# A planned order with corrected durations, two more weight slots, and one unit for the exponentials of an SSD group

## The chip, the cores and the metric

The kernel runs on one core of a Trainium2 chip. The metric is the device time of one execution in microseconds (us); the median of three runs of the kernel before is 1147.33 us (1146.54 to 1148.89). The engines are named as the profile names them: PE (TensorE, matmuls), DVE (VectorE), ACT (ScalarE), POOL (GpSimd), and SP, whose queue issues every DMA of this kernel.

## The reference, cut to what matters

One sequence of 256 tokens with 1024 features passes through two layers in fp32. A layer is a SwiGLU feed-forward block, a mixer, and a second feed-forward block, each followed by a layer norm. The mixer of the first layer ("hyb") joins a gated delta rule with an mLSTM; that of the second ("ssd") is a chunked state-space scan.

```python
for l in range(DEPTH):
    x = _layer_norm(DN_ALPHA * x + 0.5 * _swiglu(x, ffn_pre_w_gate[l], ...))
    mix = _hybrid_mixer(x, ...) if l % 2 == 0 else _ssd_mixer(x, ...)
    x = _layer_norm(DN_ALPHA * x + mix, ...)
    x = _layer_norm(DN_ALPHA * x + 0.5 * _swiglu(x, ffn_post_w_gate[l], ...))
```

Three pieces of the mixers matter below. The delta rule solves with a unit lower triangular matrix per head and chunk, `triangular_solve(lower + eye, rhs)`. The mLSTM gates its output, `o_b = sigmoid(mo) * h`. The scan needs for each head the decay between all pairs of positions of a chunk, `seg = exp(where(causal, a_cum[i] - a_cum[j], -inf))`, the decay to the chunk's end `d_end`, and `e_cum = exp(a_cum)`.

## The kernel before, in words

**Numbers.** All weights are fp32 in memory. A block of weights arrives as a tile `raw` (128 rows of 1024 or 1040 columns, about half a megabyte); ACT rounds it into `hi` and DVE forms the rest `lo`; each product is then three matmuls (hi with hi, lo with hi, hi with lo) of 128x256 to 128x512 columns. So every block costs one cast on ACT and one subtraction on DVE beside its matmuls on PE.

**Who sets the order.** The class `Plan` records every operation of the program and, in `order()` (L354), plays a list scheduler over them with durations of its own (`_cost`, L269), due times (`rank`, L321) and a model of the DMA queue. What it finds becomes the instruction order of each engine, and also gives each tile its slot: tiles of the kind `m4`, which hold `raw`, `hi`, `lo`, and most wide intermediates, share `NSLOT` slots (L33). `emit` (L476) then issues all of them from one line, so in the profile every instruction stands at L488 and is told from others by its tiles. Engines run their queues strictly in that order; a table of numbers in the scheduler therefore changes the program without a change in the mathematics.

**The hyb mixer around the triangular solve.** `k_dot` gives the products of keys; DVE multiplies them into `Ls` (two halves, 16 instructions). SP writes `Ls` to scratch memory (`scrdl`) and reads it back as `ab`, the 16x16 diagonal blocks, 64 rows each (L1084 to L1085). `block_inverse` (L1283) inverts them on DVE, and begins with a product of `ab` with a constant mask and a difference from the identity, both columns of the constant array `cst`. Beside it runs the mLSTM: its weights `mE` are multiplied on PE with `mv`, DVE divides by the denominator `md` and gates with `sg` into `my`, and PE transposes `my` for the output projection (written `tr<-ident,my`). In the recorded order DVE does the block inverse ahead of `md` and `my`.

**The ssd mixer.** There are four groups of eight heads. `decays(gi)` (L1417) loads, for a group, two tiles `abc` (a half of the sequence each, broadcast over the partitions from scratch), and ACT turns them into decays: eight `Relu` instructions with a per-head bias per tile (so that what would be above the diagonal is cut off), then `Exp`. Two small exponentials belong to it: `sea` (once) and `sde` (per group). ACT holds one table of functions at a time: `Exp` needs another than `silu`, and the instruction ACT_TABLE_LOAD stands wherever the order changes from one to the other. `chunk(gi)` (L1469) multiplies `abc` with `cb` (from the feature-major `bf` and `cf`, which come out of a convolution `cv` and a silu), transposes `xf`, forms `xd`, `xe` and `y` on DVE, multiplies `xe` into a state, which ACT copies to `hst`, and adds the product of `hst` with `cf`.

Of the kernel before, what the change touches and what calls it, by code (L numbers as in the profile page):

```python
# [19 lines left out]
P = 128  # L20
D = 1024
S = 256
# [10 lines left out]
NSLOT = 40  # L33
# [7 lines left out]
C_EYE16 = 896  # L41
C_LOW16 = 1152
C_N = 1408


def _const_array():
# [9 lines left out]
    c[:, C_LOW16:C_LOW16 + 256] = np.tril(np.ones((16, 16), np.float32), -1).reshape(1, 256)  # L56
    c[:, C_EYE16:C_EYE16 + 256] = np.eye(16, dtype=np.float32).reshape(1, 256)
# [3 lines left out]
SB_SLOTS = {"m4": (NSLOT, WMAX), "m2": (6, 512), "m1": (6, 256), "tiny": (12, 16), "tiny96": (12, 96)}  # L61
# [12 lines left out]
class Buf:  # L74


    def __init__(self, n, tag, shape, dtype, name):
# [6 lines left out]
        self.ops = []  # L84
        self.place = None
# [99 lines left out]
class Plan:  # L185
# [83 lines left out]
    def _cost(self, op, method, a, k):  # L269
# [12 lines left out]
        elif q == "SP":  # L282
# [5 lines left out]
            op.rate = 410 if isinstance(src, bass.AP) and not src.tensor.name.startswith("scr") else 300  # L288
        else:
# [20 lines left out]
            elif q == "ACT":  # L310
                op.busy += 180 + .85 * n + 60 * scal - LAG["ACT"] + (186 if "accum_out" in k else 0)
# [38 lines left out]
    MARGIN, LEAD = 1000, 0  # L350
# [3 lines left out]
    def order(self):  # L354
# [18 lines left out]
        dma = 0.0  # L373
# [12 lines left out]

        def start(o, q):
            t = max(ready[o, q], clock[q])
            if o.news:
# [23 lines left out]
        while len(out) < len(ops):  # L413
            best = None
            for q in QUEUES:
# [4 lines left out]
                now = [(o.prio + 2 * switch(o, q), o.n, t, o) for t, o in can if t <= t0]  # L420
                mine = min(now)
                for p, n, t, o in sorted((o.prio + 2 * switch(o, q), o.n, t, o) for t, o in can if t > t0):
# [24 lines left out]
            if q == "SP":  # L447
                first = max(dma, t + busy)
                dma = first + max(350, o.bytes / o.rate)
                end = dma + 2000 + self.MARGIN * o.raw  # L450
# [6 lines left out]
            o.done, o.begun, o.on = end, t, q  # L457
            out.append(o)
# [32 lines left out]
class Net:  # L491
# [92 lines left out]
    def consts(self):  # L584
# [7 lines left out]
        self.ones = self.one([32, S], F32, name="ones")  # L592
        nc.gpsimd.memset(self.ones, 1.0)
# [277 lines left out]
    def hyb(self, g, b, last=False):  # L871
# [24 lines left out]
        ones = self.ones[0:8]  # L896

# [38 lines left out]
        with hp():  # L936
            sin = t96(12, "sin")
            V.tensor_copy(sin[:, :, 0:8], gt[:, :, 8:16])
            V.tensor_scalar_mul(sin[:, :, 8:12], gt[:, :, 20:24], -1.0)
# [15 lines left out]
            rw = self.m4([8, 4, S], nm="hrows")  # L955
            for half in range(2):
# [130 lines left out]
        mq = self.m4([P, 2, S], nm="mq")  # L1087
# [3 lines left out]
        mk = self.m4([P, 2, S], nm="mk")  # L1091
# [3 lines left out]
        for pr in range(2):  # L1095
            for q in range(2):
# [5 lines left out]
                qk = V.tensor_mul(e, e, ps[:, 0:3 * P])  # L1102
        with hp():
# [533 lines left out]
```

## Time and profile before

| | |
|---|---|
| median of 3 runs | 1147.33 us |
| profiled execution, device time | 1146.67 us |
| its span in the profile | 1144.9 us |
| PE busy | 1112.7 us (97%) |
| DVE busy | 758.5 us (66%) |
| ACT busy | 587.9 us (51%) |
| mean granted clock of PE | 0.995 |

The profiled execution lies 0.66 us below the median, and 1.8 us of its device time lie outside its span. Busy time is time in which an engine had an instruction under way; since matmuls overlap in the pipeline, a busy PE need not be at its best rate. The granted clock is 1.00 at 2.4 GHz and 0.50 at 1.2 GHz. Times in rows count from the start of the span.

### The profile page before, as it was taken

How to read it: one execution, taken by the hardware profiler on the slowest of the kernel's cores; microseconds unless marked ns; L12 is line 12 of the kernel's file. 1: busy time of each engine (PE TensorE's matmuls, PEld its weight loads, DVE VectorE, ACT ScalarE, POOL GpSimd, SP SyncE). 2: the span in 40 equal slices, each digit the busy share in tenths (PEclk: the TensorE clock that was granted, in tenths of full speed). 3: DMA queues.
4: the chain of work that ended last, by engine and by line, in shares of the span. 5: the costliest groups of instructions: out<-in, count | busy, mean ns of one | idle time of the engine just before them, and what ended most of it. 6: DMA issues, size and time to landing. Idle time of an engine off the chain costs nothing.

```text
span 1144.9 us, 19783 instructions
## 1 busy us (share of the span) xinstructions
PE 1112.7 (97%) x8118; PEld 1041.5 (91%) x8118; DVE 758.5 (66%) x1242; ACT 587.9 (51%) x890; POOL 26.2 (2%) x53
## 2 busy tenths in 40 slices
PE   7999999998999999999999999999999999999996
PEld 7999998998998999999899999899998779999995
DVE  6945456787969955455865545696788889655425
ACT  6755443593423544344354444379889636444410
POOL 0000000000000000000000000000011220000000
PEclk9999999998999999999999999999999999999999
DMA  9766554648424555565465555465545446655601
GB/s 358 288 212 205 196 183 133 191 171 214 186 102 159 197 190 192 191 206 174 148 223 200 188 197 187 134 217 187 185 146 178 149 163 243 218 172 187 212 19 37
DMA packets 75955, 210.02 MB, mean 183 GB/s; under 512 B 13580, under 2 KB 26328, under 8 KB 75864
## 3 DMA queue, kind: packets, MB, share of 16 engines
q1 hardware_dynamic: 75864, 208.76, 54.3%
q8 instruction: 63, 1.03, 0.4%
q14 instruction: 28, 0.23, 0.1%
HBM read 204.23 MB, written 4.50 MB: 182 GB/s over the span
## 4 chain that ended last, share of the span: by engine, by line
PE 81%; DVE 8%; ACT 6%; DMA 3%; issue 1%; SPq 0%; DVEq 0%; ACTq 0%
PE gu L488 46%; PE acc L488 32%; PE tr L488 3%; DVE cv L488 2%; DMA raw<-in_wgu 2%; DVE lo L488 2%; ACT L488 2%; ACT abc L488 1%; DVE x L488 1%; ACT cv L488 1%; DMA ab<-scrdl 1%; ACT Ls L488 1%; ACT hi L488 0%; DVE ry L488 0%; DMA x<-in_x 0%
## 5 line engine op out<-in xcount | busy, mean ns | idle before, releaser
L488 DVE TENSOR_TENSOR lo<-raw,hi 128x1024 fp32r<-128x1024 f32 (+2 forms) x358 | 428.8, 1216 | 145.0 <-ACT hi L488 141.4
L488 ACT CAST hi<-raw 128x1024 fp32r<-128x1024 f32 (+2 forms) x358 | 370.1, 1045 | 203.0 <-DMA raw<-in_wgu 125.1
L488 PE MATMUL gu<-xl,hi 128*128 128x256 f32 x1216 | 341.9, 281 | 0.0
L488 PE MATMUL gu<-xh,hi 128*128 128x256 f32 x1216 | 341.2, 281 | 0.0
L488 PE MATMUL gu<-xh,lo 128*128 128x256 f32 x1216 | 341.1, 281 | 0.0
L488 PEld LDWEIGHTS gu<-xh,hi 128*128 128x128 f32 x1216 | 229.0, 188 | 1.0
L488 PEld LDWEIGHTS gu<-xl,hi 128*128 128x128 f32 x1216 | 228.9, 188 | 1.1
L488 PEld LDWEIGHTS gu<-xh,lo 128*128 128x128 f32 x1216 | 229.1, 188 | 0.0
L488 PE MATMUL acc<-hi,h 128*128 128x512 f32 (+1 forms) x748 | 228.7, 381 | 0.0
L488 PEld LDWEIGHTS acc<-hi,h 128*128 128x128 f32 x748 | 138.1, 188 | 27.5
L488 PE MATMUL acc<-lo,h 128*128 128x512 f32 (+1 forms) x374 | 142.1, 380 | 0.0
L488 ACT ACTIVATE sg<-gu 128x256 f32<-128x256 f32 (+1 forms) x100 | 35.9, 359 | 183.3 <-PE gu L488 183.1
L488 DVE TENSOR_TENSOR hf<-sg,gu 128x256 f32<-128x256 f32 (+1 forms) x100 | 38.7, 388 | 108.2 <-ACT sg L488 108.0
L488 PE MATMUL acc<-xh,hi 128*128 128x256 f32 x320 | 92.7, 290 | 0.0
L488 PE MATMUL acc<-xl,hi 128*128 128x256 f32 x320 | 90.5, 283 | 0.0
L488 PE MATMUL acc<-xh,lo 128*128 128x256 f32 x320 | 90.2, 282 | 0.0
L488 PEld LDWEIGHTS acc<-lo,h 128*128 128x128 f32 x374 | 70.3, 188 | 13.1
L488 PE MATMUL acc<-hi,xh 128*128 128x260 f32 x224 | 64.0, 286 | 0.0
L488 PE MATMUL acc<-hi,xl 128*128 128x260 f32 x224 | 63.4, 283 | 0.4 <-DVE xl L488 0.4
L488 PE MATMUL acc<-lo,xh 128*128 128x260 f32 x224 | 63.3, 283 | 0.0
L488 PEld LDWEIGHTS acc<-xh,hi 128*128 128x128 f32 x320 | 61.0, 190 | 0.6 <-issue 0.2
L488 DVE TENSOR_TENSOR h<-hf,h 128x256 fp32r<-128x256 f32 x76 | 32.3, 425 | 44.0 <-ACT h L488 44.0
(272 smaller groups left out, 1445.5 us busy)
## 6 DMA issues: line engine op xcount, KB each, us to landing
raw<-in_wgu SPq DMA_DIRECT2D x176, 512.0 KB, 5.0
raw<-in_wd SPq DMA_DIRECT2D x88, 512.0 KB, 5.8
raw<-in_ssd_fm SPq DMA_DIRECT2D x24, 512.0 KB, 5.7
raw<-in_ssd_tm SPq DMA_DIRECT2D x16, 520.0 KB, 4.5
raw<-in_hyb_fm SPq DMA_DIRECT2D x16, 512.0 KB, 5.2
raw<-in_ssd_out SPq DMA_DIRECT2D x16, 512.0 KB, 5.7
raw<-in_hyb_tm SPq DMA_DIRECT2D x12, 520.0 KB, 4.4
raw<-in_hyb_out SPq DMA_DIRECT2D x8, 512.0 KB, 6.8
```

Of the source, the lines that this page charges most:

```text
L488: getattr(engines[o.on], method)(*map(real, a), **{x: real(v) for x, v in k.items()})
```

## The change

The planner gets other numbers: how long scratch transfers take by the size of their pieces, a model in which SP's transfers land one behind the other, a charge for ACT's scalar operands, a larger margin for weights, and a wait for a PSUM bank that another engine still uses. `NSLOT` goes from 40 to 42. Room for that comes from the constants: the 16x16 identity and mask leave `cst` and become an input of their own, `cst16`, loaded on SP into a tile `c16` shortly before the block inverse; the constant tile of ones becomes two small ones that POOL fills where they are used; `mq` and `mk` share a tile. And in `decays`, the exponentials of a group (both halves, `sde`, and `sea` in the first group) are one unit that ACT runs without anything between, with the product `de * dt` behind it. No matmul is added or removed.

```diff
-NSLOT = 40
+NSLOT = 42
...
-C_EYE16 = 896
-C_LOW16 = 1152
-C_N = 1408
+C_N = 896
...
+def _const16():
+
+    c = np.stack([np.eye(16, dtype=np.float32), np.tril(np.ones((16, 16), np.float32), -1)])
+    return np.broadcast_to(c.reshape(1, 512), (P, 512)).copy()
...
-SB_SLOTS = {"m4": (NSLOT, WMAX), "m2": (6, 512), "m1": (6, 256), "tiny": (12, 16), "tiny96": (12, 96)}
+SB_SLOTS = {"m4": (NSLOT, WMAX), "m2": (6, 512), "m1": (6, 256), "tiny": (12, 16), "tiny96": (11, 64)}
...
-            op.rate = 410 if isinstance(src, bass.AP) and not src.tensor.name.startswith("scr") else 300
+            far = [v for v in (out, src) if isinstance(v, bass.AP)][0]
+            if far.tensor.name.startswith("scr"):
+                piece = 4 * far.ap[-1][1]
+                op.rate = 82 if piece <= 64 else 228 if isinstance(src, View) else 291
...
+            for b in o.banks:
+
+                for e, end in b.seen.items():
+                    if e != q:
+                        t = max(t, end + HAND[e][q])
...
-        ones = self.ones[0:8]
-
...
-            V.tensor_scalar_mul(sin[:, :, 8:12], gt[:, :, 20:24], -1.0)
+            neg = V.tensor_scalar_mul(sin[:, :, 8:12], gt[:, :, 20:24], -1.0)
...
+            ones = self.m1([8, S], nm="ones")
+            with self.plan.behind(neg):
+                G.memset(ones, 1.0)
...
-        mq = self.m4([P, 2, S], nm="mq")
+        mqk = self.m4([P, 4, S], nm="mqk")
+        mq = mqk[:, 0:2]
...
-        mk = self.m4([P, 2, S], nm="mk")
+        mk = mqk[:, 2:4]
...
+        c16 = self.m2([P, 512], nm="c16")
+        with self.plan.behind(qk):
+            DQ(c16, self.ap["cst16"])
         with hp():
-            self.block_inverse(ab, c, dd)
+            self.block_inverse(ab, c16, dd)
...
-        ea = t32(1, "sea")
-        A.activation(ea[:, 0, :], nam[:, 1, :], AF.Exp, scale=-1.0)
-        ea = ea[:, 0, :]
+        ea = t32(1, "sea")[:, 0, :]
         de = t32(1, "sde")[:, 0, :]
         M = {}
 
         def decays(gi):
+            sl = slice(gi * 8, gi * 8 + 8)
             for half in range(2):
                 bc = self.m4([P, 8, P], nm="abc")
                 DQ(bc, ds_[half][gi * 8:gi * 8 + 8, :].partition_broadcast(P))
                 if half == 0:
-                    sl = slice(gi * 8, gi * 8 + 8)
                     V.tensor_add(de[:, sl], bc[:, :, P - 1], nam[:, 0, sl])
-                    A.activation(de[:, sl], de[:, sl], AF.Exp)
-                    V.tensor_mul(de[:, sl], de[:, sl], dt[:, 0, sl])
                 for r in range(8):
                     h = gi * 8 + r
                     A.activation(bc[:, r, :], bc[:, r, :], AF.Relu, scale=-1.0, bias=pam[:, half, h:h + 1])
-                A.activation(bc, bc, AF.Exp, scale=-1.0)
                 M[gi, half] = bc
+            with self.plan.group():
+                if gi == 0:
+                    A.activation(ea, nam[:, 1, :], AF.Exp, scale=-1.0)
+                A.activation(de[:, sl], de[:, sl], AF.Exp)
+                for half in range(2):
+                    A.activation(M[gi, half], M[gi, half], AF.Exp, scale=-1.0)
+            V.tensor_mul(de[:, sl], de[:, sl], dt[:, 0, sl])
```

The program after has 22 ACT_TABLE_LOAD instructions, where before it had 38; 24 of those before and 10 of those after stand in the ssd mixer. SP has one DMA more, POOL one memset more.

**First place: SP behind the products `Ls` in hyb.** Before, SP's queue reads (`scrdl` is `Ls` on its way out, `ab` the diagonal blocks on their way in, one for each half, `raw` a block of weights):

```order
111 L488 DMA scrdl_65<-Ls_2580 128x8x128
112 L488 DMA scrdl_66<-Ls_2684 128x8x128
113 L488 DMA raw_2904<-in_hyb_fm 128x1024
114 L488 DMA raw_2922<-in_hyb_fm 128x1024
115 L488 DMA ab_2924<-scrdl_65 64x16x16
116 L488 DMA raw_2983<-in_hyb_fm 128x1024
117 L488 DMA ab_2924<-scrdl_66 64x16x16
118 L488 DMA raw_3009<-in_hyb_fm 128x1024
119 L488 DMA raw_3051<-in_hyb_fm 128x1024
```

After, where `c_441` is the new tile `c16`:

```order
113 L507 DMA scrdl_65<-Ls_2633 128x8x128
114 L507 DMA scrdl_66<-Ls_2696 128x8x128
115 L507 DMA raw_2918<-in_hyb_fm 128x1024
116 L507 DMA ab_2927<-scrdl_65 64x16x16
117 L507 DMA c_441_2938<-in_cst 128x512
118 L507 DMA raw_2982<-in_hyb_fm 128x1024
119 L507 DMA ab_2927<-scrdl_66 64x16x16
120 L507 DMA raw_3018<-in_hyb_fm 128x1024
121 L507 DMA raw_3074<-in_hyb_out 128x1024
```

Behind the two `scrdl` one block of weights stands ahead of the first `ab` and not two; between the two `ab` stand the new constant and one block. On DVE three `gbc` and three `mE` multiplications that stood ahead of `Ls` now stand behind it, and the block inverse still stands ahead of `my`.

**Second place: PE at the transposes of `my` in hyb.** Before:

```order
1854 L488 MATMUL tr_3118<-mv_339_1966,mE_2662 128x129 x2
1855 L488 MATMUL tr_3123<-mv_339_1966,mE_2740 128x129 x2
1856 L488 MATMUL tr_3133<-mv_339_1966,mE_2662 128x129 x4
1857 L488 MATMUL tr_3145<-ident,my_3141 128x128
1858 L488 MATMUL tr_3148<-mv_339_1966,mE_2740 128x129
1859 L488 MATMUL tr_3145<-ident,my_3141 128x128
1860 L488 MATMUL tr_3148<-mv_339_1966,mE_2740 128x129 x2
1861 L488 MATMUL tr_3145<-ident,my_3141 128x128 x2
1862 L488 MATMUL tr_3148<-mv_339_1966,mE_2740 128x129
1863 L488 MATMUL acc_3168<-xh,hi_2877 128x256
1864 L488 MATMUL acc_3168<-xl,hi_2877 128x256
```

After (the left-out rows repeat the three products once more):

```order
1858 L507 MATMUL tr_3120<-mv_339_1952,mE_2669 128x129 x2
1859 L507 MATMUL tr_3124<-mv_339_1952,mE_2734 128x129 x2
1860 L507 MATMUL tr_3132<-mv_339_1952,mE_2669 128x129 x4
1861 L507 MATMUL tr_3146<-mv_339_1952,mE_2734 128x129 x4
1862 L507 MATMUL acc_3163<-xh,hi_2843 128x256
1863 L507 MATMUL acc_3163<-xl,hi_2843 128x256
1864 L507 MATMUL acc_3163<-xh,lo_2916 128x256
...
1868 L507 MATMUL tr_3173<-ident,my_3157 128x128 x4
```

All twelve products with `mE` and six matmuls of the next weights now stand ahead of the first transpose of `my`; before, four of these products stood among and behind the transposes, and the weights came last.

**Third place: ACT in the ssd mixer, from the decays of the second group to the copy `hst` of the first.** Before:

```order
601 L488 ACT_TABLE_LOAD
602 L488 ACTIVATE sde<-sde 128x8
603 L488 ACT_TABLE_LOAD
604 L488 ACTIVATE zs_9122<-acc_9072 128x244
605 L488 ACTIVATE zs_8230<-acc_9072 128x16
606 L488 ACTIVATE abc_8968<-abc_8968,spam 128x128 x4
607 L488 ACTIVATE zs_9122<-acc_9099 128x244
608 L488 ACTIVATE zs_8230<-acc_9099 128x16
609 L488 CAST hi_9147<-raw_8985 128x1024
610 L488 ACT_TABLE_LOAD
611 L488 ACTIVATE abc_8968<-abc_8968 128x1024
612 L488 COPY hst_9179<-gu_9170 128x512
```

After; directly ahead of these rows stand one table load, `sde` and the exponentials of both tiles `abc`:

```order
593 L507 ACT_TABLE_LOAD
594 L507 ACTIVATE zs_8237<-acc_9047 128x260
595 L507 ACTIVATE zs_9127<-acc_9080 128x244
596 L507 ACTIVATE zs_8237<-acc_9080 128x16
597 L507 CAST hi_9130<-raw_8978 128x1024
598 L507 CAST hi_9144<-raw_8999 128x1024
599 L507 ACTIVATE zs_9127<-acc_9110 128x244
600 L507 ACTIVATE zs_8237<-acc_9110 128x16
601 L507 CAST hi_9162<-raw_9078 128x1024
602 L507 CAST hi_9168<-raw_9125 128x1024
603 L507 CAST hi_9189<-raw_9148 128x1040
604 L507 COPY hst_9194<-gu_9185 128x512
```

The two table loads and the exponential that stood just ahead of `hst` are gone from there, and five casts of weights stand ahead of it, of which one stood there before. On PE two things move with it: behind the first two transposes of `bf` at the head of the ssd scan stand 24 matmuls of the next weights, spread among the transposes of `bf`, ahead of the first products with `cf` (before none did), and in the second group 18 matmuls stand between the transposes of `xf` and the product with `xe` (before none did). In the third group four transposes of `y` stand there. On ACT, in the first group, all sixteen `Relu` instructions, one table load and the whole unit stand ahead of the convolution that gives the third and fourth `bf`; before, four `Relu` instructions did. In feed-forward blocks several `tr<-ident,hf` stand six matmuls later.

## Rows read from the trace of the kernel before

**Rows 1.** The page: busy time with share and instructions, then the chain that ended last.

```profile
PE 1112.7 (97%) x8118; PEld 1041.5 (91%) x8118; DVE 758.5 (66%) x1242; ACT 587.9 (51%) x890; POOL 26.2 (2%) x53
...
PE 81%; DVE 8%; ACT 6%; DMA 3%; issue 1%; SPq 0%; DVEq 0%; ACTq 0%
```

**Rows 2.** Waits of PE: total, times, longest, in us.

```profile
PE tr L488 <- DVE my L488: 4.5, 1, 4.5
PE gu L488 <- DVE xe L488: 2.7, 2, 1.7
PE gu L488 <- ACT hst L488: 2.7, 3, 1.9
PE tr L488 <- ACT cf L488: 1.8, 2, 1.5
...
PE tr L488 <- ACT kf L488: 0.9, 1, 0.9
PE tr L488 <- DVE hf L488: 0.8, 2, 0.6
```

**Rows 3.** Stretches in hyb: PE, PEld, DVE, ACT, POOL busy (instructions), PEclk, DMA share, GB/s.

```profile
250.00:260.00 10.00, 10.00 (x87) 9.85 (x87) 10.00 (x22) 6.31 (x8) 0.00 (x0) 1.00 0.82 234
...
269.40:274.00 4.60, 0.11 (x2) 0.12 (x1) 4.46 (x14) 0.36 (x1) 0.00 (x0) 0.82 0.19 21
274.00:279.20 5.20, 5.20 (x25) 5.20 (x26) 3.56 (x17) 0.59 (x1) 0.00 (x0) 0.51 0.90 193
```

**Rows 4.** Timeline of PE around the transposes of `my`: start, us, instruction, count [idle before].

```profile
267.47 1.95 PE L488 MATMUL tr<-mv,mE 128*128 128x129 f32 x16
273.91 0.45 PE L488 MATMUL tr<-ident,my 128*128 128x128 f32 x1 [4.49 <-DVE my L488]
```

**Rows 5.** Timeline of DVE from the end of `Ls` to `my`.

```profile
251.51 1.11 DVE L488 SCALAR_TENSOR_TENSOR Ls<-tr,rkkb,Ls 128x128 f32<-128x128 f32 x4
...
259.66 2.35 DVE L488 TENSOR_TENSOR lo<-raw,hi 128x1024 fp32r<-128x1024 f32 x2
264.26 0.43 DVE L488 TENSOR_TENSOR ab<-ab,cst 128x256 f32<-128x256 f32 x1 [2.25 <-DMA ab<-scrdl]
...
273.41 0.61 DVE L488 SCALAR_TENSOR_TENSOR my<-tr,md,sg 128x128 f32<-128x128 f32 x2
...
274.13 0.61 DVE L488 SCALAR_TENSOR_TENSOR my<-tr,md,sg 128x128 f32<-128x128 f32 x2
```

**Rows 6.** DVE ahead of `Ls`: two of the `gbc` multiplications.

```profile
229.99 0.61 DVE L488 SCALAR_TENSOR_TENSOR gbc<-gbc,gm,cst 128x128 f32<-128x128 f32 x2
```

**Rows 7.** SP's issues in that stretch: start, us of issue.

```profile
250.62 2.44 SPq L488 DMA_DIRECT2D scrdl<-Ls  x2
253.16 1.72 SPq L488 DMA_DIRECT2D raw<-in_hyb_fm  x2
254.97 0.70 SPq L488 DMA_DIRECT2D ab<-scrdl  x1
...
256.45 0.73 SPq L488 DMA_DIRECT2D ab<-scrdl  x1
```

**Rows 8.** DMA issues from 250 to 266: count, KB each, median us to landing.

```profile
ab<-scrdl SPq DMA_DIRECT2D x2, 64.0 KB, 6.4
```

**Rows 9.** Timeline of ACT ahead of `hst`, first group of ssd.

```profile
829.79 1.05 ACT L488 CAST hi<-raw 128x1024 fp32r<-128x1024 f32 x1
830.86 1.28 ACT L488 ACT_TABLE_LOAD   x1
832.16 1.06 ACT L488 ACTIVATE abc<-abc 128x1024 f32<-128x1024 f32 x1
833.12 0.57 ACT L488 COPY hst<-gu 128x512 f32<-128x512 f32 x1
```

**Rows 10.** Groups of ACT: busy us, mean ns, idle before.

```profile
L488 ACT ACT_TABLE_LOAD x38 | 48.8, 1283 | 3.4 <-DVE cv L488 2.1 <-PEq L1626 0.7
```

**Rows 11.** ACT in the third group: seven `Relu`.

```profile
854.39 2.16 ACT L488 ACTIVATE abc<-abc,spam 128x128 f32<-128x128 f32 x7
```

More of the change, by code (lines that the diff above doesn't have):

```diff
@@ L84, in __init__ @@
         self.ops = []
+        self.seen = {}
         self.place = None
@@ L310, in _cost @@
             elif q == "ACT":
-                op.busy += 180 + .85 * n + 60 * scal - LAG["ACT"] + (186 if "accum_out" in k else 0)
+                op.busy += 180 + .85 * n + 60 * scal - LAG["ACT"] + (40 if scal and not ps else 0) + (186 if "accum_out" in k else 0)
                 f = a[2] if method == "activation" and len(a) > 2 else None
@@ L349 @@
     PE_DUE = False
-    MARGIN, LEAD = 1000, 0
+    SWITCH = 2
+    MARGIN, LATE, LEAD = 1500, 200, 0
     WAIT = 2
@@ L372, in order @@
         clock["SP"] = 700.0
-        dma = 0.0
+        dma, row = 0.0, 0
         table = None
@@ L385, in order @@
                 offer(o)
+        for o in ops:
+            o.banks = list({v.buf for _, a, k in o.calls for v in list(a) + list(k.values())
+                            if isinstance(v, View) and v.buf.psum})
         def start(o, q):
             t = max(ready[o, q], clock[q])
+            for b in o.banks:
+                for e, end in b.seen.items():
+                    if e != q:
+                        t = max(t, end + HAND[e][q])
             if o.news:
@@ L419, in order @@
                 t0 = max(min(t for t, _ in can), clock[q] + 1)
-                now = [(o.prio + 2 * switch(o, q), o.n, t, o) for t, o in can if t <= t0]
+                now = [(o.prio + self.SWITCH * switch(o, q), o.n, t, o) for t, o in can if t <= t0]
                 mine = min(now)
-                for p, n, t, o in sorted((o.prio + 2 * switch(o, q), o.n, t, o) for t, o in can if t > t0):
+                for p, n, t, o in sorted((o.prio + self.SWITCH * switch(o, q), o.n, t, o) for t, o in can if t > t0):
                     if p + self.WAIT * (t - t0) < mine[0] and t - t0 < self.FRAC[q] * mine[3].busy:
@@ L447, in order @@
             if q == "SP":
-                first = max(dma, t + busy)
-                dma = first + max(350, o.bytes / o.rate)
-                end = dma + 2000 + self.MARGIN * o.raw
+                took = max(350, o.bytes / o.rate)
+                row = 1 if t + busy >= dma else row + 1
+                dma = max(t + busy + 2100 + took, dma + took + (1300 if row == 2 and took > 900 else 0))
+                end = dma + self.LATE
             if q == "ACT" and o.exps is not None:
@@ L457, in order @@
             o.done, o.begun, o.on = end, t, q
+            for b in o.banks:
+                b.seen[q] = end
             out.append(o)
@@ L591, in consts @@
         self.x = self.one([P, 2, D], F32, name="x")
-        self.ones = self.one([32, S], F32, name="ones")
-        nc.gpsimd.memset(self.ones, 1.0)
         self.mhalf = self.one([P, 1], F32, name="mhalf")
@@ L1364, in ssd @@
             DQ(vec, self.ap["ssd_vec"].partition_broadcast(P))
-        ones = self.ones[:, 0:P]
         t32 = lambda n, nm: self.one([P, n, NH], F32, name=nm)
@@ L1399, in ssd @@
         rw = self.m1([NH, S], nm="srow")
+        ones = self.m1([NH, P], nm="ones")
+        with self.plan.behind(soft):
+            G.memset(ones, 1.0)
         ds_ = [self.scratch([NH, P], f"ds{half}") for half in range(2)]
@@ L1576, in _layouts @@
     f = lambda a: np.ascontiguousarray(np.asarray(a))
-    o = {"cst": _const_array(), "ident": np.eye(P, dtype=np.float32), "x": f(i["x"])[0]}
+    o = {"cst": _const_array(), "cst16": _const16(), "ident": np.eye(P, dtype=np.float32), "x": f(i["x"])[0]}
     gu, dn = [], []
```

8 lines of the change are left out of this document (3 added, 5 removed).

## The prediction

> **What bounds the kernel now.** I read the page's busy times first: PE has an instruction under way for 97% of the span and carries 81% of the chain that ended last, so a gain must come from what PE loses; ACT and DVE, with 51% and 66%, matter only where PE waits for them [rows 1]. Second, the waits of PE, grouped by what ended them: 4.5 us for `my` in hyb, once; in ssd 2.7 us for `xe`, 2.7 for `hst` and 1.8 for `cf`, together 7.2; 0.9 for `kf` and 0.8 for `hf` [rows 2]. Third, the stretches around the longest: PE does almost nothing from 269.4 to 274.0, and its granted clock over these 4.6 us is 0.82, so for (1 - 0.82) / 0.5 of them, 1.7 us, it was already at 1.2 GHz: it fell about 2.9 us into the idle time. In the next 5.2 us it is 0.51 and 25 matmuls are done; at clock 1.00, 87 matmuls took 10.0 us, 0.115 us each [rows 3]. At that rate 25 cost 2.9 us: the low clock cost up to 2.3 us. A difference of 0.2% (2.3 us) is about what a measurement of this kernel can tell from no change.
>
> **The change part by part.** No matmul is added, so each term is a wait of PE that shrinks or grows.
>
> *`my` in hyb.* The chain before: DVE has finished its last `lo` at 262.0, sits idle 2.25 us until the second `ab` has landed, inverts the blocks, and gives the first `my` in time for PE at 273.91 [rows 4, 5]. What the order changes: three `gbc` and three `mE` multiplications go from ahead of `Ls` to behind it. Two `gbc` take 0.61 us [rows 6]; the `mE` ones are of like width, so six take about 1.85 us (estimate), and `Ls`, done at 252.6, would be done at about 250.75 [rows 5]. DVE's own arrival at the inverse stays: what is taken from ahead of `Ls` is done behind it, plus one copy of 0.3, so 262.3 and not 262.0. The second `ab` now counts. It was issued at 256.45, and the row that waited for it began at 264.26, 7.8 us later; the median `ab` took 6.4 us for only 64 KB [rows 5, 7, 8]. Its issue can move by the whole 1.85 us, or, since one `raw` that needs a slot still stands before each `ab` on SP, by about 1.0 (the issue of the two `raw` lasted until 254.9 and the first `ab` was issued right behind [rows 7]). The new constant, 256 KB, is queued between the `ab`, and one `raw` of 512 KB fewer ahead of them; I set these against each other. So it lands between 262.4 and 263.3; I take 262.7, since a slot count of 42 frees `raw` sooner rather than later, and the inverse starts 1.55 us earlier. The reordered `md` costs 0.1. First `my`: 273.91 - 1.55 + 0.1 = 272.45.
>
> PE arrives before at 273.91 - 4.49 = 269.42 [rows 4]. It now has four products with `mE` more (16 took 1.95 us, so 0.5) and six matmuls (0.7) ahead of it [rows 3, 4], less the 0.45 that I take from `kf` below: 270.15. First wait 2.3 us. The four transposes stand together, and the second pair of `my` comes 0.72 us after the first [rows 5], of which two transposes hide about 0.2: second wait 0.5. Together 2.8 and not 4.5: gain 1.7. The inverse still stands ahead of `my`, so a wait of some size stays; the bounds are 0 (the second `ab` not earlier, its wait merely split) and 4.5.
>
> *The clock behind it.* An idle time of 2.3 us ends before the 2.9 at which the clock fell here [rows 3]. Then the half-clock stretch is gone. I take 2.0 of its 2.3, as PE would wait for the second `my` there at either clock; bounds 0, if the wait comes out near 3 us, and 2.3.
>
> *`kf`.* Its silu on ACT stands earlier, but six covering matmuls stand behind it and not before (0.7). Of the 0.9 us [rows 2] I take half, 0.45; bounds -0.7 and 0.9.
>
> *ssd, `cf`.* PE now has 24 matmuls, 2.8 us, ahead of the products with `cf` [rows 3], more than the whole 1.8 [rows 2]. But ACT has all sixteen `Relu` (0.31 each, 4.9 [rows 11]), a load (1.28) and the unit (two exponentials of 1.06 and two small ones, 2.5) ahead of the convolution of the third and fourth `bf`: 8.7 us where 1.2 stood, though the later of these 7.5 us, and two loads more, stood there anyway before `cf`. What it delays are the `bf` that PE now needs among those 24. Gain 0; bounds -1.5 and 1.8.
>
> *ssd, `hst`, first group.* Ahead of `hst` stood a load and an exponential, 2.3 us, and one cast of 1.05 [rows 9]; now five casts, 5.2 us, but ACT reaches them 2.6 us earlier, as two loads fewer stand between [rows 9, 10]. 3.4 against 5.2 - 2.6: gain 0 for the longest wait, 1.9 [rows 2], as SP can hold up a cast; bounds -2 and 1.9.
>
> *ssd, `xe`, second and third group.* Waits of 1.0 and 1.7 [rows 2]. In the second group 18 matmuls, 2.1 us, stand in front: 1.0 gained, but three casts ahead of the next `hst` give back 0.2. In the third, four transposes, 0.4 us: 0.4 gained. Sum 1.2; bounds -0.5 and 2.7.
>
> On ACT's table loads: the 14 fewer in ssd save 14 x 1.28 = 18 us of ACT's time [rows 10], none of it PE's except as counted. Behind the load at 830.86 the exponential starts at 832.16, 0.02 us after its end, and ahead of the load the cast ends at 830.84 [rows 9]: no further time goes with a switch. The Trainium skill, "ScalarE: Activation LUTs", section "What ACT_TABLE_LOAD costs", puts a load at about 1.28 us, as here, and adds about 1.38 us of drain, 2.66 us for each switch. By that figure the 14 would be worth 37 us of ACT's time, and `hst` of the first group would come 1.4 us earlier (estimate): the sum would be 1.4 us lower. This trace speaks against it.
>
> *`hf`.* Six matmuls more, 0.7 us, cover waits of 0.6 and 0.2: gain 0.8, bounds 0 and 0.8 [rows 2, 3].
>
> *At nothing:* the memsets run on POOL, busy 2% [rows 1]; uncovered they would cost their own tenths of a microsecond. `mqk`, the smaller `cst` and the smaller tiles change room only. Bank waits, rates and margins act through the order alone.
>
> *Sum:* 1.7 + 2.0 + 0.45 + 0 + 0 + 1.2 + 0.8 = 6.15 us. Against the profiled execution, 1146.67 - 6.15 = 1140.5; that execution lies 0.66 us below the median, so 1141.2 us.
>
> **The rivals.** *A, the clock still falls.* The second `ab` lands as late as before or the first wait comes out near 3 us; then 2.0 and about 1.2 of the 1.7 are lost, and with ssd at zero the sum is 0.45 + 0.5 + 0.8 = 1.75: 1145.6 us. For it: 7.8 us from issue to use for 64 KB shows how much a queue in flight decides; against it: three half-megabyte blocks were under way there, now two and a quarter one [rows 7].
>
> *B, nothing moves.* PE is at 97% and its other waits merely change places [rows 1]; at a sum between -2 and 2, 1147 us. Against it: the longest wait has a cause that the order does move.
>
> *C, slower: ACT's queue in ssd.* An engine runs in order, so five casts ahead of one `hst`, three ahead of another, and the sixteen `Relu` with the unit ahead of `bf` each can make PE wait for what is not late now. Price, with each cast 1.05 and nothing won back: 2.1 more for the first `hst`, 3.1 for the second, and for `cf` 7.5 - 2.8 = 4.7, together 9.9, less the 4.95 that hyb and `hf` give: about 5 slower, 1152 us. It decides from where ssd's waits, now 7.2, pass 14.5. For it: ACT is the fuller engine there. Against it: it has 18 us less to do.
>
> *D, more.* All 7.2 us of ssd's waits and the rest of `my` (2.8) go: 10 - 1.2 = 8.8 beyond the sum, 1132.4 us. For it: freed time on ACT. Against it: `xe` needs PE's transposes and DVE in any order, and `my` still stands behind the inverse.
>
> **How the numbers follow.** The forecast, 0.45, with a range of its own from 1138.5 to 1144; A 0.18; B 0.12; C 0.10; D, in whole or half, 0.15. Faster by over 0.2% (below 1145.0) takes the forecast, D and half of A: 0.69. Within 0.2%: the other half of A and three quarters of B, 0.18. Slower: C and what is left of B, 0.13. The range reaches from three quarters of the way to D, 1134.5, to just past B, 1148.0; below it about 0.07 is left out, above it about 0.11. Predicted: 1141.2 us.
>
> **What would show it right or wrong.** Right: in the waits of PE `my` at 2 to 3 us in total, no stretch at clock 0.5 between 260 and 290, `hf` gone, `xe` below 1.5, `hst` and `cf` about as before; `ab` landed 1 to 2 us earlier than 264.2; 22 table loads of 1.28 us. Wrong: `my` at over 4 us with the low clock again (A); waits of PE in ssd of over 14 us, with ACT's casts the last to end ahead of `hst`, or `bf` among the waits (C); waits that are gone and a time that is not lower, which would mean that PE's rate in stretches without waits has changed.

## The result and the profile after

The changed kernel takes 1132.62 us (median of 4 runs, 1132.19 to 1133.07), the kernel before beside it 1147.77 us: a ratio of 0.9868, with a 95% interval of 0.9851 to 0.9885. That is 15.1 us less where 6.15 were forecast, and below the stated range (1134.5 to 1148.0). The profiled execution took 1132.26 us with a span of 1130.5 us, 14.4 us less than that of the kernel before.

The page of the changed kernel, busy times and the chain that ended last, answers to [rows 1]:

```profile
PE 1108.1 (98%) x8118; PEld 1038.5 (92%) x8118; DVE 756.0 (67%) x1242; ACT 570.8 (50%) x874; POOL 25.8 (2%) x54
...
PE 89%; DVE 5%; ACT 2%; DMA 2%; issue 1%; SPq 0%; DVEq 0%; ACTq 0%
```

PE's share of the chain rose from 81% to 89%: what left it is DVE, ACT and DMA. The waits of PE after, to be held against [rows 2]:

```profile
PE tr L507 <- DVE y L507: 2.3, 2, 1.6
...
PE tr L507 <- DVE my L507: 0.7, 1, 0.7
PE gu L507 <- DVE xe L507: 0.6, 1, 0.6
PE tr L507 <- ACT kf L507: 0.5, 1, 0.5
PE gu L507 <- issue: 0.5, 1, 0.5
...
PE tr L507 <- ACT bf L507: 0.2, 1, 0.2
```

The row for `y` of the kernel before, which [rows 2] leave out:

```profile
PE tr L488 <- DVE y L488: 0.6, 1, 0.6
```

`my` went from 4.5 to 0.7; `hst` (2.7), `cf` (1.8) and `hf` (0.8) are gone from the list; `xe` went from 2.7 to 0.6; `y` went up from 0.6 to 2.3. No idle time of PE behind the first 20 us is longer than 1.6 us.

A sum over each trace tells what kind of time was saved. Of PE's time to the end of its last matmul I take the idle times over 0.15 us (those of the first 20 us left out), and half of the time at the low clock in which PE wasn't idle (of the 6.83 us at 1.2 GHz before, 1.60 lie in the idle time ahead of `my` and are counted there):

| profiled execution | PE's last matmul | idle | lost to the clock | the rest |
|---|---|---|---|---|
| before | 1135.78 | 16.05 | 2.62 | 1117.11 |
| after | 1121.46 | 6.43 | 0 | 1115.03 |
| difference | 14.32 | 9.62 | 2.62 | 2.08 |

The idle time saved is 3.75 us at `my`, 4.8 in ssd, 0.8 at `hf`, 0.4 at `kf`, 0.35 at `x`, less a new one of 0.5. The 2.1 us of the rest stand in no idle time, and I found no one place for them. The stretches of the changed kernel (PE, PEld, DVE, ACT, POOL busy, clock, DMA share, GB/s) show the two regions:

```profile
250.00:300.00 50.00, 48.63 (x409) 47.49 (x405) 46.42 (x115) 28.58 (x45) 0.00 (x0) 1.00 0.83 243
...
800.00:850.00 50.00, 49.86 (x410) 48.49 (x409) 39.28 (x62) 40.62 (x87) 3.98 (x10) 1.00 0.53 174
850.00:900.00 50.00, 47.88 (x324) 42.19 (x323) 44.80 (x66) 33.79 (x63) 12.55 (x25) 1.00 0.53 182
```

Around `my` the clock is at 1.00 throughout, where it fell to 0.51 [rows 3]. From 800 to 850 PE is idle for 0.1 us.

**hyb.** DVE and SP from the end of `Ls` to `my`, two timelines of the changed kernel, and the answer on the tile `ab`:

```profile
249.64 1.12 DVE L507 SCALAR_TENSOR_TENSOR Ls<-tr,rkkb,Ls 128x128 f32<-128x128 f32 x4
250.67 0.87 DVE L507 SCALAR_TENSOR_TENSOR gbc<-gbc,gm,cst 128x128 f32<-128x128 f32 x3
...
260.80 1.22 DVE L507 TENSOR_TENSOR lo<-raw,hi 128x1024 fp32r<-128x1024 f32 x1
261.94 0.42 DVE L507 TENSOR_TENSOR ab<-ab,c 128x256 f32<-128x256 f32 x1
...
271.02 0.61 DVE L507 SCALAR_TENSOR_TENSOR my<-tr,md,sg 128x128 f32<-128x128 f32 x2
```

```profile
254.64 0.33 SPq L507 DMA_DIRECT2D raw<-in_hyb_fm  x1
255.06 0.59 SPq L507 DMA_DIRECT2D ab<-scrdl  x1
```

```profile
DMA to landing us min/median/max: 5.9/6.1/6.3
```

`Ls` ends at 250.7, 1.85 us earlier than in [rows 5], as forecast. The second `ab` is issued 1.4 us earlier than in [rows 7] and lands 5.9 us later, at 260.9; DVE, which has no idle time ahead of `ab` now, reaches it at 261.94. So the wait of DVE for `ab`, 2.25 us in [rows 5], is gone, and DVE's own work sets the start of the inverse. Why this transfer landed faster isn't shown. PE then:

```profile
267.23 2.84 PE L507 MATMUL tr<-mv,mE 128*128 128x129 f32 x24
...
271.52 1.21 PE L507 MATMUL tr<-ident,my 128*128 128x128 f32 x4 [0.74 <-DVE my L507]
```

All 24 instructions for the twelve products stand ahead of `my`. A product is two instructions of 0.12 us each, where my forecast had counted one. The four transposes begin at 271.52, 271.69, 272.15 and 272.40; the third and the fourth begin 0.05 us behind the end of their `my` on DVE (272.09 and 272.35). Other transposes follow one another at 0.11 us (783.20, 783.31, 783.42), so about 0.5 us of the 1.21 is a second wait for `my`, which the row counts as busy.

**ssd.** ACT of the changed kernel ahead of the first `hst`, to be held against [rows 9], then PE at the same place, before and after:

```profile
809.90 1.28 ACT L507 ACT_TABLE_LOAD   x1
811.20 0.21 ACT L507 ACTIVATE sde<-sde 128x8 f32<-128x8 f32 x1
811.31 2.00 ACT L507 ACTIVATE abc<-abc 128x1024 f32<-128x1024 f32 x2
813.32 1.28 ACT L507 ACT_TABLE_LOAD   x1
...
817.43 2.98 ACT L507 CAST hi<-raw 128x1024 fp32r<-128x1024 f32 x3
820.28 0.62 ACT L507 COPY hst<-gu 128x512 f32<-128x512 f32 x1
```

```profile
833.74 1.12 PE L488 MATMUL gu<-hst,cf 128*128 128x512 f32 x2 [1.92 <-ACT hst L488]
```

```profile
821.55 1.08 PE L507 MATMUL gu<-hst,cf 128*128 128x512 f32 x2
```

In spite of five casts ahead of it, `hst` is done at 820.90, and PE gets to its product at 821.55. So `hst` is done 12.8 us earlier than before (833.69), and PE comes to it 10.3 us earlier (831.82 before). The load of a table still takes 1.28 us with the next instruction 0.02 us behind its end (809.90 + 1.28, 811.20).

In the third group, where before PE waited 1.7 us for `xe`, the changed kernel has:

```profile
872.92 0.63 PE L507 MATMUL tr<-ident,y 128*128 128x128 f32 x4 [1.55 <-DVE y L507]
874.12 1.10 PE L507 MATMUL gu<-xe,btm 128*128 128x512 f32 x2 [0.57 <-DVE xe L507]
```

The four transposes of `y` that now stand ahead of `xe` wait themselves: 2.1 us together where 1.7 stood.

### The profile page after: what moved, and what is told of

It is laid out like the page before. It is cut to its first block, busy times and chain, and to the rows that moved or that the text cites. A ratio compares the mean times of both kernels' runs of the same rounds, so it can differ in the third digit from the quotient of the medians.

```text
span 1130.5 us, 19808 instructions
## 1 busy us (share of the span) xinstructions
PE 1108.1 (98%) x8118; PEld 1038.5 (92%) x8118; DVE 756.0 (67%) x1242; ACT 570.8 (50%) x874; POOL 25.8 (2%) x54
## 4 chain that ended last, share of the span: by engine, by line
PE 89%; DVE 5%; ACT 2%; DMA 2%; issue 1%; SPq 0%; DVEq 0%; ACTq 0%
PE gu L507 49%; PE acc L507 37%; PE tr L507 3%; DMA raw<-in_wgu 1%; DVE lo L507 1%; DVE x L507 1%; DVE cv L507 1%; DMA gbc<-scrdg 1%; ACT abc L507 1%; DMA raw<-in_ssd_fm 1%; ACT L507 0%; ACT cv L507 0%; ACT Ls L507 0%; DVE bt L507 0%; DVE mE L507 0%
## 5 line engine op out<-in xcount | busy, mean ns | idle before, releaser
L507 PEld LDWEIGHTS acc<-xl,hi 128*128 128x128 f32 x320 | 60.5, 189 | 0.2 <-issue 0.2
```

What stands on the lines that cost most here:

```text
L507: getattr(engines[o.on], method)(*map(real, a), **{x: real(v) for x, v in k.items()})
```

## The experiments

All are changes of the changed kernel or of the kernel before; each is compared with runs of the kernel before on its own chip, whose medians lie between 1147.5 and 1148.3 us.

### Which part: the unit, the numbers, the slots

**e1, no unit.**

```diff
-            with self.plan.group():
-                if gi == 0:
-                    A.activation(ea, nam[:, 1, :], AF.Exp, scale=-1.0)
...
+                    A.activation(de[:, sl], de[:, sl], AF.Exp)
+                    V.tensor_mul(de[:, sl], de[:, sl], dt[:, 0, sl])
...
+                A.activation(bc, bc, AF.Exp, scale=-1.0)
```

> The changed kernel with the exponentials of a group written as before, each where it was, planned anew with the new numbers and 42 slots. Theory (ACT's time freed by fewer table loads took the waits for hst, xe and cf away): these waits come back, PE loses about 5 us between 780 and 900, so about 1137.5 us; hyb stays as in the changed kernel, with a wait for my under 1.5 us. Rival (the new order, not the unit, took them away): 1132 to 1134 us although some 12 table loads more are issued.

1133.78 us, ratio 0.9881 [0.9865, 0.9898], an interval that holds the 0.9868 of the whole change. The answer on ACT's groups in e1 (busy us, mean ns) against the changed kernel's 22 loads of 28.2 us:

```profile
L507 ACT ACT_TABLE_LOAD x34 | 43.6, 1283 | 2.8 <-DVE cv L507 1.5 <-PEq L1650 0.7
```

With twelve loads more, 15.4 us of ACT's time, the program takes about 1 us more by the medians, and the two intervals overlap. The rival holds for `hst` and `cf`: their waits are gone without the unit too. `xe` waits 2.8 us in three places, but `y` only 0.7, so that ssd is idle for little more than in the changed kernel.

**e2, the old numbers.**

```diff
-            far = [v for v in (out, src) if isinstance(v, bass.AP)][0]
...
+            op.rate = 410 if isinstance(src, bass.AP) and not src.tensor.name.startswith("scr") else 300
...
-    MARGIN, LATE, LEAD = 1500, 200, 0
+    MARGIN, LATE, LEAD = 1000, 200, 0
...
-                dma = max(t + busy + 2100 + took, dma + took + (1300 if row == 2 and took > 900 else 0))
-                end = dma + self.LATE
+                first = max(dma, t + busy)
+                dma = first + max(350, o.bytes / o.rate)
+                end = dma + 2000 + 1000 * o.raw
```

The charge on ACT and the bank wait go too, as in the diff of e11 below.

> The changed kernel with 42 slots and the unit, but with the planner's old numbers: old rates and old model of SP's queue, margin 1000, no charge for scalar operands, no wait for a PSUM bank. Theory (the numbers moved the work around Ls and ab and so took the wait for my away): my waits 3 us or more again, the clock falls, hf waits again; ssd stays good: about 1139 us. Rival (slots and unit give it all): 1132 to 1134 us.

1150.24 us (1143.59 to 1152.08), ratio 1.0018 [1.0000, 1.0035]: the gain is gone altogether. In its profiled execution (1144.60 us) PE waited 3.6 us for `my`, 3.4 for `xe`, 2.5 for `y`, 2.1 for `qf`. So ssd isn't good either under the old numbers; theory and rival both missed.

**e3, 40 slots.**

```diff
-NSLOT = 42
+NSLOT = 40
```

> The changed kernel with 40 slots in place of 42 and nothing else changed by hand. Theory (two slots let SP issue a block earlier, which brings the second ab earlier; the rest is order): my waits 1 to 2 us longer, 1134 to 1136 us. Rival (slots matter nowhere, as DMA is busy only about half of the time): 1132 to 1133.5 us.

1140.08 us, ratio 0.9938 [0.9921, 0.9954]. `my` waits 2.5 us, as the theory had it, but the larger loss lies elsewhere, at the third group of ssd (the timelines of PE, ACT and DVE, and stretches of that run):

```profile
878.52 2.05 PE L507 MATMUL gu<-xe,btm 128*128 128x512 f32 x2 [4.11 <-ACT hi L507]
```

```profile
864.57 4.80 ACT L507 ACTIVATE abc<-abc,spam 128x128 f32<-128x128 f32 x16
...
872.27 1.99 ACT L507 ACTIVATE abc<-abc 128x1024 f32<-128x1024 f32 x2
...
876.47 1.06 ACT L507 CAST syh<-tr 128x512 fp32r<-128x512 f32 x2
877.42 2.01 ACT L507 CAST hi<-raw 128x1024 fp32r<-128x1024 f32 x2
```

```profile
877.08 0.69 DVE L507 TENSOR_TENSOR syl<-tr,syh 128x512 fp32r<-128x512 f32 x1 [0.77 <-ACT syh L507]
877.69 0.68 DVE L507 TENSOR_TENSOR xe<-tr,sde 128x512 f32<-128x512 f32 x1
```

```profile
868.00:878.60 10.60, 6.49 (x56) 6.28 (x54) 8.69 (x15) 10.54 (x21) 0.00 (x0) 0.92 0.52 197
878.60:888.00 9.40, 9.40 (x34) 7.04 (x34) 7.11 (x10) 3.30 (x4) 0.00 (x0) 0.55 0.00 0
```

PE waits 4.1 us. The row names the cast `hi` as what ended it, but the product reads `xe` and `btm` and no `hi`; `xe` is done at 878.37, just ahead of the product's start. DVE does `xe` behind `syl`, and `syl` waits for the casts `syh` of the gated output, which stand on ACT behind sixteen `Relu`, the unit and two loads. So the chain is ACT's unit, `syh`, `syl`, `xe`, PE, and not a late cast of weights. The clock fell 2.45 us into this wait and was low for 10.2 us. It is the prediction's rival C in its mechanism, at 40 slots, though through DVE. (The 5.6 us that two expectations below give for it hold another 1.5 us of the program's first 20 us, where every run has such a wait.)

**e4, the unit with old numbers and 40 slots** (the edits of e2 and e3 together).

> Old numbers and 40 slots with the unit of exponentials; the constants lie as in the changed kernel. Theory: only ssd gains, about 5 us: 1142 us, with my waiting as before (about 4.5 us) and the low clock behind it. Rival (the unit alone gives nothing, since old numbers put the casts and convolutions wrongly around it): 1146 to 1148 us.

1154.27 us, ratio 1.0056 [1.0035, 1.0077]: a little slower than before, where the theory had 1142 us and the rival the old time. The same chain through `syh` makes PE wait 3.1 us for `xe`; `my` waits 4.5 and `ri` 2.9 us.

**e9, 41 slots; e10, 41 slots with the old SP model and rates; e11, 42 slots without the ACT charge and the bank waits.** The edits are those of e3 (with 41) and the pieces of e2; for e11:

```diff
-                op.busy += 180 + .85 * n + 60 * scal - LAG["ACT"] + (40 if scal and not ps else 0) + (186 if "accum_out" in k else 0)
+                op.busy += 180 + .85 * n + 60 * scal - LAG["ACT"] + (186 if "accum_out" in k else 0)
...
-            for b in o.banks:
...
-                for e, end in b.seen.items():
-                    if e != q:
-                        t = max(t, end + HAND[e][q])
```

> The changed kernel with 41 slots, planned anew. With 40 the time was 1140.1 us, 2 us of it in hyb and 5.6 at one late cast in ssd. Theory (a slot is worth what the order built on it happens to leave waiting, no steady price for each): 1132 to 1140 us with waits in places of its own. Rival (each slot brings SP's blocks earlier by as much): about 1136 us, half of the way, with the wait for my near 1.6 us.

> The kernel of the run with 41 slots, but with the planner's old rates of scratch transfers and old model of SP's queue; the charge on ACT and the bank wait stay new. Theory (of the new numbers, those of the DMA side move Ls, ab and the abc tiles and carry most of the gain): 4 us or more above the run with 41 slots, my waiting 2 us or more. Rival (the numbers for ACT and the banks carry it): within 1.5 us of the run with 41 slots.

> The changed kernel with 42 slots, the new rates and the new model of SP's queue, but without the charge of 40 for scalar operands on ACT and without the wait for a PSUM bank. Theory: most of the gain stays, 1132 to 1136 us, with waits moved in ssd alone. Rival (these two carry it): 1139 us or more.

1142.54 us (0.9952 [0.9936, 0.9968]), 1143.27 us (0.9957 [0.9939, 0.9976]) and 1147.56 us (0.9993 [0.9974, 1.0011]). With 41 slots, slower than with 40, PE waits 4.1 us for `xe` behind `syh`, as with 40; theory and rival both had less. With the old SP model `my` waits 4.3 us, but that wait behind `syh` isn't there: the two times agree, as the rival had it, and their causes don't. Without the ACT charge and the bank waits `my` waits 4.4 and `xe` 3.7 us: not even the new SP model keeps `my` early by itself. The time lies with the rival; which of the two does it was not separated.

**e12, the moved constants alone** (old numbers, 40 slots, no unit).

> The old numbers, 40 slots and ungrouped exponentials, with only the constants moved (the new input and its tile, the two tiles of ones, mq and mk in one tile). The prediction put this part at nothing. Theory: the time of the kernel before within 2.3 us, 1145 to 1150 us, though the order is planned anew. Rival (the new DMA in front of the second ab costs at hyb): 1150 us or more, with my waiting over 5 us; then the run with the unit alone was slow by this and not by the unit.

1151.08 us (1146.32 to 1154.92), ratio 1.0020 [0.9999, 1.0040]. Its waits are those of before, `my` 4.5 us, plus 2.8 for `ri` and 1.3 for `qf`. The time is on the rival's side of 1150 us, but the interval holds the time of before, and `my` waits no longer. So the new DMA isn't seen to cost (the rival's place), and the order that is planned anew is no better.

**e15, the numbers alone** (with the constants; 40 slots, no unit).

> All new numbers of the planner and the moved constants, with 40 slots and ungrouped exponentials. Theory (the numbers carry the gain only together with room for two more blocks): 1138 to 1143 us, as with 40 slots and the unit (1140.1). Rival (numbers alone give it and the unit harmed at 40 slots, where one late cast behind the unit cost 5.6 us): 1133 to 1136 us.

1134.65 us, ratio 0.9879 [0.9860, 0.9898]. This is the surprise: the numbers alone (with the moved constants) give 13.7 of the 15 us. `my` waits 1.9 us, `xe` 1.8 and `qf` 1.2; the waits for `hst` and `cf` are gone, and the clock stays at 1.00 to PE's end. Together:

| new numbers | 40 slots | 42 slots |
|---|---|---|
| no unit | 1134.65 (e15) | 1133.78 (e1) |
| unit | 1140.08 (e3) | 1132.62 (the change) |

With the old numbers the three that were run took 1150 to 1154 us. The unit costs 5.4 us at 40 slots and gives at most about 1 at 42.

### Which wait: ab, hst, my

**e8, the first ab late.**

```diff
         order = self.order()
...
+        ab = [o for o in order if o.on == "SP" and name(o).startswith("ab") and not name(o).startswith("abc")]
+        order.remove(ab[0])
+        order.insert(order.index(ab[1]), ab[0])
```

> The changed kernel, its order kept, but SP issues the first ab directly ahead of the second, behind the constant and the block that stood between them. The second ab is then issued about 0.7 us later behind the same bytes. Prediction's account (the landing of the second ab sets the start of the inverse): my waits 0.7 to 1.7 us longer, 1133.3 to 1134.3 us. Theory now (the second ab landed at 260.9 and DVE reached it at 261.9, so DVE itself sets it, with 1.0 us in hand): the wait for my within 0.4 us of 0.74 and 1132.2 to 1133.2 us.

1133.72 us median of four (1132.79, 1133.19, 1134.26 and one of 1138.95), and in the profiled execution `my` waits 0.74 us as in the changed kernel. But the edit didn't make the second `ab` late: it was issued 0.2 us later (255.28 against 255.06) and landed 1.1 us earlier (259.81 against 260.93), in 4.5 us instead of 5.9. So e8 doesn't test a late `ab`. That DVE sets the start rests on the changed kernel's own trace: 1.0 us between the landing and the start of the inverse, with DVE busy.

**e7, ACT later at hst.**

```diff
         order = self.order()
...
+                h = [c for c in act[:act.index(o)] if name(c).startswith("hi")][-1]
+                h.calls = h.calls + [h.calls[0]] * 3
```

> The changed kernel, its order kept, with the last cast of weights ahead of each of the four hst done four times in place of once on ACT (same result): 2.85 us more ahead of each. In the changed kernel hst is done 0.65, 0.94, 0.94 and 0.1 us before PE gets to it. Theory (ACT has under 1 us in hand at hst, so that what the order saved there, some 2 us a group, is the gain): waits of 2.2, 1.9, 1.9 and up to 2.8 us for hst, 1139 to 1141.5 us. Rival (hst has no part in the gain; the other waits set the end): under 1135 us.

1149.03 us (1146.08 to 1152.75): 16 us lost, about twice what was expected. PE's waits for `hst`, the last longer wait for `y` ahead of a fall of the clock, and the stretches around the three falls:

```profile
PE gu L513 <- ACT hst L513: 6.0, 3, 2.5
```

```profile
883.99 0.52 PE L513 MATMUL tr<-ident,y 128*128 128x128 f32 x3 [1.56 <-DVE y L513]
```

```profile
822.00:832.00 10.00, 7.49 (x40) 5.84 (x41) 6.70 (x10) 6.72 (x9) 1.68 (x5) 0.83 0.00 0
860.00:866.00 6.00, 4.39 (x18) 3.36 (x19) 4.83 (x7) 5.08 (x7) 1.17 (x4) 0.72 0.47 161
884.00:894.00 10.00, 9.43 (x39) 7.04 (x39) 8.38 (x12) 6.44 (x8) 0.00 (x0) 0.66 0.00 0
```

The waits for `hst` are the 6 us expected (less the last group's); the clock fell three times, at the end of the first two (2.5 and 1.95 us) and 1.4 us behind a wait of 1.56 us for `y`, with one of 0.6 us for `xe` close behind it; the changed kernel has the same two waits (1.55 and 0.57) without a fall. That is 13.7 us of low clock in ssd, 6.8 us lost. ACT's slack of under 1 us is real, and in this execution 7.9 us of added idle time cost 16.5 us, about double.

**e5 and e6, DVE later at my**, by 6 and 13 copies:

```diff
         order = self.order()
...
+            if method == "tensor_copy" and getattr(getattr(a[0], "buf", None), "name", "").startswith("tu"):
+                o.calls = o.calls + [o.calls[0]] * 6
```

> The changed kernel, its order kept, with the copy tu<-ti at the end of the block inverse done seven times in place of once on DVE (same result): 6 x 0.29 = 1.75 us more ahead of my. The wait for my goes from 0.74 to about 2.5 us. Theory (PE waits for DVE there with nothing in hand, and the clock is a price of its own that comes only with a longer idle time): 1132.6 + 1.75 = 1134.4 us with the clock at 1.00, about 1136 if it falls already at 2.5 us. Rival (the wait is covered elsewhere in hyb, since later transposes wait anyway): under 1133.5 us.

> The same with fourteen copies: 13 x 0.29 = 3.8 us more, so the wait for my is about 4.5 us, as long as before the change. Theory: 1132.6 + 3.8 and the half clock behind it, 1.7 to 2.3 us: 1138.1 to 1138.7 us, so 5.5 to 6.1 us in all, the share of the whole gain that hyb has. Rival (the clock's fall depends on what else PE did and not on this wait): no stretch at 0.5 and 1136.4 us.

A repeated copy takes 0.41 us and not 0.29, so the waits are 3.2 and 6.1 us. The profiled executions took 1136.49 and 1140.10 us, 4.2 and 7.8 over the changed kernel: the 2.5 and 5.35 us of waiting, and 1.7 and 2.5 for the clock. The medians (1138.75 and 1140.57) lie higher, and above what was expected, by executions with more of the low clock (mean clock down to 0.991). In e5 the clock fell 2.0 us behind the idle time, in e6 in it. The stretches of e5:

```profile
271.00:274.30 3.30, 0.08 (x1) 0.02 (x1) 3.20 (x14) 0.00 (x0) 0.00 (x0) 1.00 0.29 31
274.30:280.00 5.70, 5.56 (x31) 5.20 (x32) 4.49 (x16) 0.59 (x1) 0.00 (x0) 0.70 0.88 165
```

### What the clock is worth: PE's idle time filled in the kernel before

**e13 and e14**: PE repeats products of its own ahead of its waits, which keeps it busy and helps nobody else. The part at `my`:

```diff
         order = self.order()
...
+        for o in pe[first - 8:first]:
+            if o.calls[0][2].get("start") and o.calls[0][2].get("stop"):
+                again[o] = 8
+        for o, n in again.items():
+            o.calls = o.calls * (n + 1)
```

> The kernel before, its order kept; PE repeats four of its own products with mE eight times more each just ahead of the wait for my (32 x 0.12 = 3.9 us of work that changes no result), so that it is idle there for about 0.6 us and not 4.5. No wait becomes shorter for anyone else. Theory (the low clock is a price of its own, paid for the idle time): 2 to 2.5 us faster than before, 1145.5 us, no stretch at 0.5 behind it. Rival (the clock's fall costs nothing, since PE waits for the second my there anyway): the time of before within 0.5 us.

> As the run before it, and PE repeats work of its own also ahead of the waits for cf, the first hst, and the second and third xe, 0.5 to 1.8 us each, so that no idle time over about 0.7 us is left in ssd either. Theory (the spread of the kernel before, 1144.5 to 1152.4 us, comes from falls of the clock behind these waits in some executions): median about 1145 us and a spread under 3 us, as the changed kernel has. Rival (the spread has another source, such as transfers): a spread of 6 us or more as before.

1147.87 us (0.9998 [0.9984, 1.0013]) and 1148.42 us (0.9997 [0.9987, 1.0008]). The filling was too long: 7.2 us instead of 3.9 at `my`, so that `my` itself began 2.6 us later (measured from the transposes of `kf`), and PE came 1.5 us late at `hst`. So these two don't price the clock. The profiled execution of e14 had no low clock before PE's end, and its spread was 3.2 us (1146.86 to 1150.07).

**e16 and e17**: the same with 4 in place of 8 (and 1 in place of 2 at `hst`).

> As the run that filled the wait for my of the kernel before, with half of the filling: a product with mE turned out as two passes of 0.11 us, so eight repeats were 7.2 us, 2.2 us more than PE's idle time, and the start of my moved by that. Four repeats are 3.6 us and leave about 0.9 us idle. Theory (the low clock is a price of its own): no stretch at 0.5 there and 2.0 to 2.5 us faster than before in the fastest executions. Rival: the time of before within 0.5 us.

> As the run before it, with the filling ahead of cf, the first hst, the second and the third xe too, the one ahead of hst halved (it had overshot by 1.5 us). Theory: the clock stays at 1.00 until PE's work ends in every execution; the median is 2.5 to 4 us under that of before (2.3 for the fall that always comes, the rest for those that come in some executions), and the spread under 3 us. So of the 15 us of the change, 3 to 4 are the clock's. Rival: median within 1 us of before, the clock has no part in the gain.

In e16 the second pair of `my` is transposed 2.2 us earlier, measured from the transposes of `kf`, with the clock at 1.00 throughout that stretch: that is the price of that one fall. The whole run isn't faster (1147.76 us, 0.9994 [0.9978, 1.0010]); in its profiled execution a later wait for `hf` took 1.8 us and the clock fell behind `hst`. e17, with all places filled, is faster: 1146.09 us, 0.9979 [0.9964, 0.9995], 1144.44 to 1148.33, where before ran from 1144.65 to 1154.89. That is less than the theory's 2.5 to 4 us by the medians (1.4), and the spread of 3.9 us is wider than its 3. The interval makes the gain 0.6 to 4.1 us, most likely about 2.4. As the price of the clock this is rather a lower bound: in the profiled execution of e17 PE has 9.5 us more of work for 6.2 us less of idle time, so the filling itself costs some 3 us. For the profiled pair before and after, the table above has 2.6 us for the clock; in the medians it can be more, since the mean clock of the kernel before goes down to 0.989 in its slower executions.

## Why the prediction was wrong

**What bounds the kernel** held in the main: of the 14.3 us by which PE's last matmul moved, 9.6 are idle times of PE and 2.6 the clock; 2.1 are neither.

**The failed step is the ssd sum**, 1.2 us with `cf` and `hst` at 0. Measured, ssd's idle time fell by 4.8 us, and about 5.5 with what lies between: the changed kernel is 8.96 us ahead at the transposes of `x` at the head of ssd (743.50 against 752.46) and 14.46 ahead at those behind it (939.68 against 954.14). By place:

- `hst`, taken at 0: 2.7 us in three waits, all gone. I counted 3.4 us of ACT's work before and 2.6 net after, 0.8 in favour, and called that zero because a cast might wait for SP; no cast there waited. I left out that four `Relu` (1.27 us) no longer stand in that stretch, and when each engine comes to it: `hst` moved by 12.8 us and PE by 10.3, which turns a wait of 1.9 us into 0.65 us in hand, so the bound of +1.9 was the value. The two shorter waits (0.45 and 0.33) had no term. e7 shows how little is in hand: with 2.85 us more on ACT the waits are back.
- `cf`, taken at 0: 1.8 us, gone but for 0.2 in a wait for `bf`. I set ACT's added work against PE's cover of 2.8 us as if all of it fell on PE; 0.2 us of it did.
- `xe`, taken at 1.2: 1.0 in the second group, as forecast, but in the third 0.4 us more waiting with `y` and not 0.4 less, and 0.2 more at the last `y`.

**`my`**: the mechanism was right, the size wrong. PE's first wait is 0.74 us and not 2.3; the second, 0.5, came as forecast. The idle time gained is 3.75 us where 1.7 stood. The second `ab` landed at 260.9 and not 262.7: its issue moved by 1.4 us as bounded, and it took 5.9 us, where I had kept the 7.8 of before, as if a quarter of a megabyte less ahead of it were nothing. DVE's own arrival, 261.94, then bounds the start. And the four products with `mE` cover 1.0 us, not 0.5, since each is two instructions.

**The clock**: 2.0 us taken; 2.2 measured for this fall (e16), 2.6 by the table. But the reading under it fails: "An idle time of 2.3 us ends before the 2.9 at which the clock fell here". The clock fell 0.6 us behind an idle time of 2.5 us (e3), at the end of one of 1.95 us and 1.4 us behind one of 1.56 us (e7), and didn't at one of 3.6 us (e2). With the wait of 2.3 us that I forecast it might well have fallen; that the term came out is in part luck, since the wait is 0.74 us.

**`kf`** 0.38 for 0.45, **`hf`** 0.8 for 0.8: right. A new gain at `x`, 0.35, had no term.

**The rivals.** D, "all 7.2 us of ssd's waits and the rest of `my`", gave 1132.4 us, within 0.3 us of the result, but that is partly luck: of ssd's idle time 4.8 us went and not all, and the clock (0.6 over its term), `x` and the unplaced 2.1 us make up the difference. I gave it 0.15. Its argument against, that `xe` needs PE's transposes in any order, fell in the second group, where 18 matmuls in between cover the wait, and held in the third. C's mechanism exists (e3, e4, e7), but 42 slots and these numbers leave it none of its places. On the table loads, the trace after stays with 1.28 us a switch, and in e1 a program with twelve more of them takes only about 1 us more.

**Open**: which of the planner's numbers does it. Taking some away (e10, e11) loses 10 to 15 us, but so does one slot (e9), with other waits in other places. The margin of 1500 alone can be named: with 1000 the planner gives every engine the same order, instruction for instruction, so it does nothing. The rest act together, through an order that I can't split.

## What to carry to other kernels

When a planner's order changes, price each wait from the instant at which each engine would reach it, with slack kept as slack; don't sum added work on a side engine as if it were late. Give the case "all waits at the changed places go" its full chance when several covers are added at once. And test a kernel of several edits as a table: here one of the three edits in the title, the unit, was worth about 1 us or nothing, and at another slot count it cost 5 us. Look, too, at what an instruction reads before you believe the name of the engine that ended its wait (e3).

## What the runs showed of the hardware

The low clock comes behind the same idle times in some executions and not in others: the wait of 1.56 us for `y` in e7 was followed by a fall, the same wait of 1.55 us in the changed kernel was not, and one of the four executions of e8, whose profiled one has no idle time over 1.6 us, took 1138.95 us at a mean clock of 0.993 beside three of 1132.8 to 1134.3 at 0.997 to 0.998. The fall can cost as much as the waits: 6.8 us in the profiled execution of e7, where the added waits for `hst` were 6.0 us. Ten executions of e2 ran from 1143.6 us at a mean clock of 0.997 to 1152.1 at 0.990. The four of the changed kernel have a clock of 0.997 to 0.998 and a spread of 0.9 us; the kernel before spread over 10 us on one chip. So a removed wait of 2 to 4 us can be worth more in the median than in one profiled execution that happened to keep its clock, as that of e2 did (1144.60 us, median 1150.24).
